# Folding the MLP gain of a streaming encoder into its up weights, and moving the row scaling to ScalarE

## The chip, the cores and the metric

The kernel runs on one core of one Trainium2 chip. It is one program in one launch. The metric is device time in microseconds (us): the median of the runs of a kernel, with the lowest and highest shown beside it. One execution of each kernel was also recorded by the hardware profiler; times "in the trace" are counted from the start of that execution's span.

## The reference

One inference step of an encoder with two layers (an "A" layer with sliding-window attention, a "B" layer that attends over a shared K/V), for 1024 prompt tokens and 8 x 16 sample tokens, with a model width D of 1024 and an MLP width FF of 4096. Everything is float32. What the change touches is the MLP that ends each layer:

```python
def rmsnorm(x, g):
    y = x * rsqrt(mean(x * x, axis=-1, keepdims=True) + EPS)
    return y * g

def mlp(x, g_norm, w_up, w_down):
    return square(relu(rmsnorm(x, g_norm) @ w_up)) @ w_down

for layer in range(2):
    ...                                   # attention; its output a_p, a_s
    hp = hp + a_p @ w_o[layer]            # prompt rows
    hs = hs + a_s @ w_o[layer]            # sample rows
    hp = hp + mlp(hp, g_mlp[layer], w_up[layer], w_down[layer])
    hs = hs + mlp(hs, g_mlp[layer], w_up[layer], w_down[layer])
```

`g_mlp` has one gain for each of the 1024 channels. It multiplies the normalized row along its channels; the channels are also the rows of `w_up`.

## The kernel before

Rows of tokens are held in nine tiles of 128 tokens: 0 to 7 for the prompt, 8 (`ST`) for the sample tokens. Float32 products are made from float32r matrix multiplies: each operand is split into a rounded part and a remainder (`split`: a cast, on ScalarE as a rule, L109, then a subtraction, on VectorE as a rule, L115), and three multiplies (`mm3`, L727 to L729) stand for one.

Each layer has four stages.

1. `attention(layer)`: projections, scores, probabilities, values, and part of the output projection. At its step 10 a load is issued on SP that broadcasts the layer's `g_mlp` to 128 partitions (L1685, tile `gb`, 128x1024). Tiles named in `kept` get their norm at the end of this stage (L1730).
2. `wo_phase(layer)`, the row phase: the rest of the output projection (`ps_wo`, L157 to L159), the residual added in VectorE (L665), and `norm`: ScalarE sums the squares (L617), VectorE makes mean and EPS of it (L619), GpSimd takes the power -0.5 (L621), and VectorE multiplies the row in place by that number and by `gb` (L622). Then the rows are transposed for the MLP. The MLP of the prompt is multiplied by a Strassen-like scheme of seven products over quarters, so for each pair of row tiles (t, t + 4) GpSimd makes four sums and differences of half rows (`S`, L681 to L684), and `T` makes seven groups of four 128x128 transposes on TensorE (`turn`, L674) into one bank `ps_n` each, which ScalarE casts and VectorE subtracts into the operands `sx`. The row phase has four PSUM banks for `ps_wo` and three for `ps_n`.
3. `mlp_up`: 16 blocks of 256 columns of `w_up`. Per block two raw weight tiles (`raw[0]`, `raw[1]`, 128x4x256, upper and lower half of the channels) are loaded by SP (L755, three buffers), split into `wq`, combined in place on VectorE (L787 to L790) and split again. Seven products follow (`ps_x`, `ps_y`, `ps_z`), with the sample tokens' product (`ps_s`) in between. ScalarE copies `ps_x` out three times per block (L846, L851, L855) before the next product adds into the same bank. Block 0 runs in two halves of 256 tokens.
4. `mlp_down`: the second half of the MLP, with the same scheme.

The order of the instructions on each engine is laid out when the kernel is built, by a planner that simulates the whole program (`schedule_with_timeline_sim=True`); at run time each engine works its queue in order. `behind` adds a few orders by hand, and `follow` keeps the products of the MLP in order on TensorE.

SBUF places follow from the order in which pools open. `raw`, `wa` and `keep` (with `gb` and the sums `s0` to `s3`) lie low and stay from the attention through the row phase; the pools of `mlp_up` open in their place. The first `hc` tiles of `mlp_up` begin where the sums `s2` and `s3` lay.

The gains of the attention norms are already folded into their weights: `prep_gains` turns all five gain vectors, the two of `g_mlp` among them, into columns of the tile `gcol` (one column for each 128 channels), which `split_g` uses as a scale for each partition.

Of the kernel before, what the change touches and what calls it, by code (L numbers as in the profile page):

```python
# [8 lines left out]
F32 = mybir.dt.float32  # L9
F32R = mybir.dt.float32r  # L10
AF = mybir.ActivationFunctionType
ALU = mybir.AluOpType
# [4 lines left out]
P = 128  # L17
D = 1024
KC = D // P
# [56 lines left out]
class Build:  # L76
# [537 lines left out]
    def norm(self, small, junk, x):  # L614
        nc = self.nc
        ssq = small.tile([P, 1], F32, tag="mssq", name="mssq")
        nc.scalar.activation(junk, x, AF.Square, accum_out=ssq)  # L617
        ms = small.tile([P, 1], F32, tag="mms", name="mms")
        nc.vector.tensor_scalar(ms, ssq, 1.0 / D, EPS, ALU.mult, ALU.add)  # L619
        rs = small.tile([P, 1], F32, tag="mrs", name="mrs")  # L620
        nc.gpsimd.tensor_tensor(rs, ms, self.mhalf[:, 0:1], ALU.pow)  # L621
        return nc.vector.scalar_tensor_tensor(x, x, rs, self.gb, ALU.mult, ALU.mult)  # L622

    def wo_phase(self, layer, sx, x8, wo):
        nc = self.nc
        with ExitStack() as st:
            self.psum_pools(st, f"wo{layer}", dict(m=(4, 1), g=(3, 1)), dict(m="m", n="g"))
            work = self.pool(st, f"wow{layer}")
            small = self.pool(st, f"wosm{layer}", 2)
            osp, xs = {}, {}  # L630
# [63 lines left out]
            z = 0  # L694
# [64 lines left out]
    def mlp_up(self, layer, sx, x8, rp, raw0):  # L759
        nc = self.nc  # L760
        tt = nc.vector.tensor_tensor
        with ExitStack() as st:
# [11 lines left out]
            def weights(b):  # L774
                raw = self.up_raw(layer, rp, b) if b else raw0
                quad = []
                for h in range(2):
                    q = [
                        take(f"q{b % 2}{v}") if h else rp[0].tile([P, 4, FB], F32R, tag=f"q{v}", name="wq")
                        for v in range(2)  # L780
                    ]
                    self.split(q[0], q[1], raw[h])
                    quad.append(q)
                b11, b12 = raw[0][:, :, 0:P], raw[0][:, :, P:FB]
                b21, b22 = raw[1][:, :, 0:P], raw[1][:, :, P:FB]
                t = b11, b22, b12, b21
                tt(t[0], b12, b11, ALU.subtract)  # L787
                tt(t[2], b22, b12, ALU.subtract)
                tt(t[1], b22, t[0], ALU.subtract)
                tt(t[3], b21, t[1], ALU.subtract)  # L790
                ts = [None] * 4
                for n in (1, 2, 0, 3):
                    w = take(f"t{b % 2}{n}")
                    self.split(w[:, 0], w[:, 1], t[n])
                    ts[n] = w[:, 0], w[:, 1]
                q = lambda h, n: [quad[h][v][:, :, n * P : n * P + P] for v in range(2)]
                return quad, [q(0, 0), q(1, 0), q(1, 1), ts[3], ts[0], ts[1], ts[2]]
# [77 lines left out]
            for b in range(NFB):  # L875
# [7 lines left out]
                s = [hp.tile([P, 512], F32, tag="h", name="hs", bufs=HB) for _ in range(3)]  # L883
# [284 lines left out]
    def run(self):  # L1168
        nc, tc = self.nc, self.tc
        I = self.ins  # L1170
# [7 lines left out]
        with ExitStack() as top:  # L1178
# [49 lines left out]
            for layer in range(2):  # L1228
                with ExitStack() as st:
                    low = st.enter_context(ExitStack())  # L1230
                    self.rawp = self.pool(low, f"raw{layer}", 2)
                    self.wa = [self.pool(low, f"wa{layer}")]
                    self.nw = 0
                    keep = self.pool(low, f"keep{layer}")
                    self.gb = keep.tile([P, D], F32, tag="gb", name="gb")
                    self.sums = lambda: [
                        keep.tile([P, 512], F32, tag=f"s{n}", name="s") for n in range(4)
                    ]
                    self.sums0 = self.sums()
                    self.kept = {}  # L1240
                    with ExitStack() as more:
                        self.wa.append(self.pool(more, f"wb{layer}"))
                        wo = self.attention(layer)
                    sx, x8, rp = self.up_pools(st, layer)
                    raw0 = self.up_raw(layer, rp, 0)
                    self.wo_phase(layer, sx, x8, wo)
                    low.close()
                    self.mlp_up(layer, sx, x8, rp, raw0)
                self.mlp_down(layer, y if layer else lambda t: self.xd[t])
# [24 lines left out]
    def attention(self, layer):  # L1274
        nc, I = self.nc, self.ins
# [17 lines left out]
        with ExitStack() as st:  # L1293
# [292 lines left out]
            def weave(*fs):  # L1586
                for z in zip(*fs):
                    run(z)
# [57 lines left out]
            wo = [None, None]  # L1646
# [34 lines left out]
            for s in range(2 * NT):  # L1681
                u = U(s)
                next(u)
                if s == 10:
                    nc.sync.dma_start(self.gb, I["g_mlp"][layer].partition_broadcast(P))  # L1685
                q, n = s + 2, s + 3
                f = work_of(2 * s)
                if s == 7:
                    f.insert(2, lambda: Q2(ST, 1))
                a, b, c, d = cfg["up"]  # L1690
# [17 lines left out]
                f = work_of(2 * s + 1)  # L1708
# [20 lines left out]
            for xt in self.kept.values():  # L1729
                n = self.norm(small, self.scratch([P, D], mybir.dt.bfloat16, "junk"), xt)  # L1730
# [76 lines left out]
```

## Time and profile before

| | |
|---|---|
| median of 3 runs | 2391.8 us |
| lowest and highest | 2388.46, 2393.51 us |
| the profiled execution, its own time | 2387.86 us |
| its span | 2386.1 us |
| granted TensorE clock over the span | 0.996 of full speed |
| TensorE (PE) busy | 2313.9 us, 97% |
| VectorE (DVE) busy | 1627.6 us, 68% |
| ScalarE (ACT) busy | 1216.5 us, 51% |
| GpSimd (POOL) busy | 540.8 us, 23% |

The span is what the profiler saw from the first to the last instruction; the execution's own time has 1.8 us around it. "Busy" counts the time in which at least one instruction ran on the engine; PEld is TensorE's loading of weights, which runs beside its multiplies. Windows are given as start:end in us of the trace. In a row of instructions, "x3" says that three were merged into one row.

### The profile page before, as it was taken

What the parts mean: (1) busy time and instruction counts of PE and PEld (TensorE: products, weight loads), DVE (VectorE), ACT (ScalarE), POOL (GpSimd) and SP (SyncE); (2) the same over time, 40 slices, a digit from 0 to 9 for tenths busy, and PEclk for the clock granted to TensorE, in tenths of its full rate; (3) what the DMA queues carried; (4) which work ended last, traced back from release to release, by engine and by line L of the source; (5) the groups of instructions that cost most, each with busy time, mean ns of one, the idle gap of its engine ahead of it and who ended that gap; (6) DMA issues with size and microseconds to landing.
All of it is one profiled execution on the core that took longest, in us unless ns stands there. A gap on an engine that the chain in (4) does not pass through costs nothing.

```text
span 2386.1 us, 33438 instructions
## 1 busy us (share of the span) xinstructions
PE 2313.9 (97%) x11621; PEld 1931.7 (81%) x11621; DVE 1627.6 (68%) x3002; ACT 1216.5 (51%) x2423; POOL 540.8 (23%) x828
## 2 busy tenths in 40 slices
PE   7998999899999999999999999998999999999999
PEld 6787877788888878888778788887888888888887
DVE  6788786655565776776577876877555565777674
ACT  3777674555555432332267666665555555323321
POOL 4334332311221100000333444444111211000000
PEclk9999999999999999999999999999999999999999
DMA  7335545343443964333653655554443445734332
GB/s 258 119 108 169 170 146 200 129 146 126 157 146 123 356 213 149 119 128 109 232 153 112 198 166 167 168 168 169 142 142 129 158 145 203 274 133 159 117 113 115
DMA packets 217529, 383.78 MB, mean 161 GB/s; under 512 B 50248, under 2 KB 124944, under 8 KB 210192
## 3 DMA queue, kind: packets, MB, share of 16 engines
q1 hardware_dynamic: 194288, 305.08, 38.9%
q0 software_dynamic: 21776, 71.84, 7.8%
q10 hardware_dynamic: 1296, 4.72, 0.5%
q8 instruction: 92, 1.51, 0.3%
q14 instruction: 77, 0.63, 0.1%
HBM read 245.42 MB, written 135.09 MB: 159 GB/s over the span
## 4 chain that ended last, share of the span: by engine, by line
PE 79%; DVE 7%; DMA 7%; ACT 3%; issue 2%; POOL 1%; SPq 1%; ACTq 0%; DVEq 0%; POOLq 0%
PE ps_x L727 9%; PE ps_x L729 9%; PE ps_x L728 9%; PE ps_y L729 7%; PE ps_y L728 7%; PE ps_y L727 7%; PE ps_mm L198 3%; PE ps_mm L200 3%; PE ps_mm L199 3%; PE ps_tr L305 2%; PE ps_mm L157 1%; PE ps_mm L158 1%; PE ps_mm L159 1%; PE ps_s L729 1%; PE ps_s L728 1%
## 5 line engine op out<-in xcount | busy, mean ns | idle before, releaser
L109 ACT CAST w<-r 128x2048 fp32r<-128x2048 f32 x56 | 107.1, 1913 | 325.2 <-PE ps_y L729 213.0
L727 PE MATMUL ps_x<-w,s 128*128 128x512 f32 x512 | 199.6, 390 | 4.2 <-DVE hc L866 2.1
L729 PE MATMUL ps_x<-w,s 128*128 128x512 f32 x512 | 199.4, 389 | 0.0
L728 PE MATMUL ps_x<-w,s 128*128 128x512 f32 x512 | 199.3, 389 | 0.0
L198 PE MATMUL ps_mm<-w,hh 128*128 128x512 f32 x432 | 172.5, 401 | 7.3 <-POOL w L166 3.2
L200 PE MATMUL ps_mm<-w,hl 128*128 128x512 f32 x432 | 172.1, 399 | 1.6 <-DVE hl L115 0.8
L199 PE MATMUL ps_mm<-w,hh 128*128 128x512 f32 x432 | 170.9, 397 | 1.3 <-DVE w L171 1.1
L109 ACT CAST s<-s 128x2048 fp32r<-128x2048 f32 x56 | 107.1, 1913 | 118.1 <-DMA s<-hd 109.3
L115 DVE TENSOR_TENSOR w<-r,w 128x2048 fp32r<-128x2048 f32 x56 | 128.2, 2290 | 51.0 <-ACT w L109 51.0
L727 PE MATMUL ps_x<-sx,w 128*128 128x512 f32 (+1 forms) x408 | 157.9, 387 | 3.9 <-ACT hc L846 3.0
L1033 DVE TENSOR_TENSOR x<-ps_y,x 128x512 f32<-128x512 f32 x136 | 92.4, 687 | 100.8 <-PE ps_y L729 100.8
L729 PE MATMUL ps_x<-sx,w 128*128 128x512 f32 (+1 forms) x408 | 154.2, 378 | 0.0
L728 PE MATMUL ps_x<-sx,w 128*128 128x512 f32 (+1 forms) x408 | 154.1, 378 | 0.0
L109 ACT CAST w<-ru 128x512 fp32r<-128x512 f32 (+1 forms) x160 | 110.0, 708 | 85.5 <-PE ps_y L728 32.0
L729 PE MATMUL ps_y<-w,s 128*128 128x512 f32 x384 | 149.5, 389 | 0.0
L727 PE MATMUL ps_y<-w,s 128*128 128x512 f32 x384 | 149.4, 389 | 0.0
L728 PE MATMUL ps_y<-w,s 128*128 128x512 f32 x384 | 149.4, 389 | 0.0
L115 DVE TENSOR_TENSOR s<-s 128x2048 fp32r<-128x2048 f32 x56 | 128.0, 2286 | 29.1 <-ACT s L109 28.9
L115 DVE TENSOR_TENSOR ptl<-ps_tr,pth 128x512 fp32r<-128x512 f32 x180 | 122.5, 685 | 24.1 <-ACT pth L109 17.8
L115 DVE TENSOR_TENSOR w<-ru,w 128x512 fp32r<-128x512 f32 (+1 forms) x160 | 126.5, 793 | 11.2 <-ACT w L109 11.1
L115 DVE TENSOR_TENSOR wq<-ru,wq 128x1024 fp32r<-128x1024 f32 x32 | 39.7, 1240 | 131.9 <-ACT wq L109 131.9
L109 ACT CAST pth<-ps_tr 128x512 fp32r<-128x512 f32 x180 | 104.9, 595 | 45.0 <-PE ps_tr L305 36.7
(280 smaller groups left out, 6579.7 us busy)
## 6 DMA issues: line engine op xcount, KB each, us to landing
s<-hd SPq DMA_DIRECT2D x56, 1024.0 KB, 4.7
ru<-in_w_up SPq DMA_DIRECT2D x64, 512.0 KB, 4.0
r<-in_w_down SPq DMA_DIRECT2D x32, 1024.0 KB, 5.8
hd<-hc POOLq DMA_DIRECT2D x128, 256.0 KB, 2.7
hd<-hs POOLq DMA_DIRECT2D x96, 256.0 KB, 2.5
x<-xd SPq DMA_DIRECT2D x41, 512.0 KB, 4.4
o<-oTd SPq DMA_DIRECT2D x52, 256.0 KB, 5.0
xd<-xo SPq DMA_DIRECT2D x18, 512.0 KB, 2.8
```

Of the source, the lines that this page charges most:

```text
L109: a = nc.scalar.copy(hi, src)
L115: return a, e.tensor_tensor(lo, src, hi.bitcast(F32), ALU.subtract)
L157: nc.tensor.matmul(ps, oh[:, k, :], w[:, 0, k, nn], start=(k == 0), stop=False)
L158: nc.tensor.matmul(ps, oh[:, k, :], w[:, 1, k, nn], start=False, stop=False)
L198: nc.tensor.matmul(ps, a, w[:, 0, k, :], start=(k == 0), stop=False)
L199: nc.tensor.matmul(ps, a, w[:, 1, k, :], start=False, stop=False)
L200: self.lp = nc.tensor.matmul(ps, b, w[:, 0, k, :], start=False, stop=(k == KC - 1))
L305: self.lp = nc.tensor.transpose(pt[:, i, :], get(i), self.ident)
L727: a = mm(ps, ah, bh, start=first, stop=False, skip_group_check=True)
L728: mm(ps, ah, bl, start=False, stop=False, skip_group_check=True)
L729: return a, mm(ps, al, bh, start=False, stop=last, skip_group_check=True)
L1033: tt(xs[t][:, N[n]], ps, xs[t][:, N[n]], ALU.add)
```

## The change

Four edits. The broadcast load of `g_mlp` and its tile `gb` go. `norm` no longer multiplies by the gain and by the row's factor on VectorE; ScalarE multiplies by the row's factor alone. The gain is multiplied into the raw up weights in place, in eight slices of 128x256 per block, before they are split: on GpSimd in block 0, on ScalarE in blocks 1 to 15. And `ps_n` in the row phase gets a fourth PSUM bank. Without `gb`, all that opens after `keep` lies 4 KB per partition lower.

```diff
@@ norm
-        return nc.vector.scalar_tensor_tensor(x, x, rs, self.gb, ALU.mult, ALU.mult)
+        return nc.scalar.activation(x, x, AF.Copy, scale=rs)
@@ wo_phase
-            self.psum_pools(st, f"wo{layer}", dict(m=(4, 1), g=(3, 1)), dict(m="m", n="g"))
+            self.psum_pools(st, f"wo{layer}", dict(m=(4, 1), g=(4, 1)), dict(m="m", n="g"))
@@ mlp_up, weights(b)
                 raw = self.up_raw(layer, rp, b) if b else raw0
                 quad = []
                 for h in range(2):
+                    for k in range(4):
+                        c = (2 + layer) * KC + h * 4 + k
+                        z, g = raw[h][:, k], self.gcol[:, c : c + 1]
+                        if b:
+                            nc.scalar.activation(z, z, AF.Copy, scale=g)
+                        else:
+                            nc.gpsimd.tensor_scalar(z, z, g, 1.0, ALU.mult, ALU.mult)
@@ run
-                    self.gb = keep.tile([P, D], F32, tag="gb", name="gb")
@@ attention
-                if s == 10:
-                    nc.sync.dma_start(self.gb, I["g_mlp"][layer].partition_broadcast(P))
```

## Rows read from the trace of the kernel before

**Rows 1.** The page: busy time of each engine, share of the span, instructions.
```profile
PE 2313.9 (97%) x11621; PEld 1931.7 (81%) x11621; DVE 1627.6 (68%) x3002; ACT 1216.5 (51%) x2423; POOL 540.8 (23%) x828
```

**Rows 2.** Windows by stage: busy us of each engine, clock, DMA share, GB/s.
```profile
core 0: us, PE busy (x) PEld busy (x) DVE busy (x) ACT busy (x) POOL busy (x), PEclk, DMA share, GB/s
...
490.00:803.00 313.00, 311.94 (x1545) 263.93 (x1544) 176.52 (x249) 174.61 (x280) 61.97 (x115) 1.00 0.45 160
...
50.00:330.00 280.00, 267.84 (x1477) 222.67 (x1475) 223.52 (x728) 202.60 (x590) 106.61 (x192) 0.99 0.47 146
...
1200.00:1560.00 360.00, 348.52 (x1915) 288.21 (x1914) 274.89 (x784) 244.64 (x682) 147.43 (x207) 1.00 0.53 162
...
425.00:450.00 25.00, 18.27 (x127) 15.01 (x125) 22.03 (x34) 16.41 (x31) 10.65 (x9) 1.00 0.34 120
...
1650.00:1680.00 30.00, 21.61 (x133) 17.82 (x132) 27.43 (x42) 19.05 (x36) 12.53 (x11) 0.89 0.30 106
...
0.00:50.00 50.00, 39.48 (x170) 32.29 (x171) 30.62 (x62) 14.13 (x29) 23.66 (x33) 1.00 0.71 255
```

**Rows 3.** TensorE's waits, 425 to 450 and then 1650 to 1680: total, times, longest.
```profile
PE ps_n L674 <- DVE sx L115: 3.4, 4, 1.9
PE ps_x L727 <- ACT hc L846: 1.4, 1, 1.4
...
PE ps_n L674 <- DVE sx L115: 6.1, 6, 2.4
```

**Rows 4.** VectorE's timeline in both tails: its row multiplications.
```profile
429.26 1.28 DVE L622 SCALAR_TENSOR_TENSOR x<-x,mrs,gb 128x1024 f32<-128x1024 f32 x1 [0.97 <-POOL mrs L621]
...
436.25 1.72 DVE L622 SCALAR_TENSOR_TENSOR x<-x,mrs,gb 128x1024 f32<-128x1024 f32 x1
...
1653.32 1.28 DVE L622 SCALAR_TENSOR_TENSOR x<-x,mrs,gb 128x1024 f32<-128x1024 f32 x1 [0.73 <-POOL mrs L621]
...
1655.33 2.28 DVE L622 SCALAR_TENSOR_TENSOR x<-x,mrs,gb 128x1024 f32<-128x1024 f32 x1
...
1663.10 1.29 DVE L622 SCALAR_TENSOR_TENSOR x<-x,mrs,gb 128x1024 f32<-128x1024 f32 x1 [0.94 <-DMA xd<-x]
```

**Rows 5.** GpSimd's timeline in the second tail: two sums of one pair.
```profile
1655.26 1.27 POOL L681 TENSOR_TENSOR s<-x 128x512 f32<-128x512 f32 x1
1656.61 2.14 POOL L682 TENSOR_TENSOR s<-s,x 128x512 f32<-128x512 f32 x1
```

**Rows 6.** Groups by form, whole span: busy us, mean ns of one, idle before.
```profile
L622 DVE SCALAR_TENSOR_TENSOR x<-x,mrs,gb 128x1024 f32<-128x1024 f32 x14 | 21.9, 1567 | 2.8 <-POOL mrs L621 1.7 <-DMA xd<-x 0.9
...
L109 ACT CAST wq<-ru 128x1024 fp32r<-128x1024 f32 x32 | 33.5, 1047 | 26.0 <-PE ps_s L729 25.9
...
L109 ACT CAST w<-ru 128x512 fp32r<-128x512 f32 x128 | 76.4, 621 | 48.6 <-DVE ru L790 23.6 <-DVE ru L787 22.1 <-DVE ru L789 2.8
...
L168 ACT ACTIVATE w<-raw,gcol 128x512 fp32r<-128x512 f32 x8 | 5.3, 720 | 0.0
...
L582 ACT ACTIVATE sp<-sp,li 128x256 f32<-128x256 f32 x16 | 8.2, 512 | 4.9 <-DVE li L397 4.8
...
L384 POOL TENSOR_SCALAR p<-p,li 128x256 f32<-128x256 f32 x112 | 53.7, 500 | 65.1 <-DVE li L397 52.3 <-ACT p L376 5.7 <-DVE nm L371 4.7
```

**Rows 7.** Timelines of ScalarE and TensorE in one up block: two copies, the products behind.
```profile
581.73 0.59 ACT L846 COPY hc<-ps_x 128x512 f32<-128x512 f32 x1 [0.19 <-DMA hd<-hs]
...
592.79 0.59 ACT L855 COPY hc<-ps_x 128x512 f32<-128x512 f32 x1 [0.50 <-PE ps_x L729]
...
584.25 0.39 PE L727 MATMUL ps_x<-sx,w 128*128 128x512 f32 x1
...
595.45 0.48 PE L727 MATMUL ps_x<-sx,w 128*128 128x512 f32 x1
```

**Rows 8.** The instructions that write or read `gb`: the load's issue on SP.
```profile
L1685 SPq DMA_DIRECT2D gb<-in_g_mlp x2: 332/336/340, 28.0 to 1166.3; - x2
```

## The prediction

> **What bounds the kernel now.** I read the page's engine shares first. TensorE is busy 2313.9 of 2386.1 us, ScalarE about half [rows 1]. So there are 72.2 us in which TensorE does not work, and a change that leaves its matrix multiplies alone can win only out of these, or add to them. The second view is the windows by stage. In the steady part of the first MLP's up projection TensorE lacks 1.1 us in 313; in the two attention stretches 12.2 us in 280 and 11.5 us in 360; but in the 25 us at the end of the first row phase it lacks 6.7 us, and in the 30 us at the end of the second 8.4 us [rows 2]. I call these two stretches the tails: the output projection runs out, and the transposes of the rows and their sums (L674) feed the first block of the MLP. In the tails VectorE is the full engine: 22.0 of 25 us, and 27.4 of 30, where ScalarE has 16.4 and 19.1 [rows 2]. The third view, TensorE's waits in the tails, names the same engine: the transposes wait for a bank of `ps_n` that VectorE's subtraction (L115) has still to read, 3.4 us and 6.1 us; the longest wait on another engine is one for ScalarE's first copy of `ps_x`, 1.4 us in each (its row reads the same in both tails) [rows 3]. In the second tail TensorE's granted clock is 0.89 of full speed, a mean of its two levels of 2.4 and 1.2 GHz; in the first it is 1.00 [rows 2]. The fourth view is VectorE's own order there: between the evictions stand the row multiplications of L622, two in the first tail (1.28 and 1.72 us), three in the second (1.28, 2.28 and 1.29 us) [rows 4]. Those are what the change takes away.
>
> **The change part by part.**
>
> *The row multiplication goes from VectorE to ScalarE.* There are 18 in all; 14 of them average 1567 ns [rows 6]. Most run while TensorE is fed by the projection, and give back nothing. The five in the tails stand in a queue that has almost no gaps: 1.28 + 1.72 = 3.0 us in the first, 1.28 + 2.28 + 1.29 = 4.85 us in the second. I count 7.85 us. No row shows the new form, 128x1024 with a scale per partition. It lies between a ScalarE cast of the same shape without one, 1047 ns, and twice the scaled 128x512, 2 x 720 ns; I take 1047 plus the 99 ns by which the scaled 128x512 exceeds the plain cast (720 - 621), 1.14 us [rows 6]. Then ScalarE would have 16.4 + 2 x 1.14 = 18.7 us in a tail of 25 - 3.0 = 22.0 us, and 19.1 + 3 x 1.14 = 22.5 us in one of 30 - 4.85 = 25.2 us. It fits, with the second tail at nine tenths. The bounds: nothing, if ScalarE sets the pace there; and all of TensorE's idle time in both tails, 15.1 us, if VectorE was the whole cause. What a clock that no longer falls would give back in the second tail stays inside this bound.
>
> The long ones among these multiplications show a collision. The 2.28 us one starts at 1655.33, beside a GpSimd sum that runs from 1655.26 for 1.27 us, and GpSimd's next sum takes 2.14 us in place of 1.27 [rows 4, 5]. Each seems to have waited about 1 us for the other. The Trainium skill (GPSIMD Engine Reference, section 8, Key points) has it that GpSimd shares its SBUF interfaces with VectorE and contends with VectorE instructions that have two SBUF inputs, as L622 has (`x` and `gb`); by that rule the sums behind it, from which four of every seven transposes are made, should also come about 1 us earlier in the second tail, and the sum would be 8.8 us instead of 7.85. I leave this 1 us out of the value, since the sums still meet other two-input work of VectorE, and keep it inside the 15.1 us.
>
> *The gain moves into the up weights.* In blocks 1 to 15 of each layer ScalarE multiplies eight slices of 128x256 in place: 240 instructions. The same form is measured at 512 ns [rows 6], so 4.1 us per block of some 22 us and 123 us in all. In the steady stretch ScalarE has 174.6 of 313 us [rows 2]; some 14 blocks bring it to 232 us, 74%. I cost this at nothing on TensorE. The cover is ScalarE's idle 138 us there; and as TensorE lacks 1.1 us in the stretch, nothing that the split weights feed is late now. If the cover is gone, what is late next is the copy of `ps_x` (L846, L851, L855), since the next product writes the same bank. L846 ends at 582.32 (581.73 + 0.59) and its product starts at 584.25, 1.93 us later; L855 ends at 593.38 and its product starts at 595.45, 2.07 us later [rows 7]. One scaling ahead of a copy is 0.5 us and disappears in this; the rival below counts from when it doesn't.
>
> In block 0 GpSimd does the same work: 8 slices per layer at 500 ns [rows 6], 4.0 us. GpSimd is busy 10.7 of 25 us and 12.5 of 30 us in the tails [rows 2], so it has the room. I take nothing; if all eight stood ahead of a tail's sums it would cost 4.0 us in that layer. Queued behind them would be the next row's power (L621) and the sums.
>
> *The fourth bank.* The transposes wait 3.4 and 6.1 us for one of three banks [rows 3]. A fourth lets TensorE run one transpose group further ahead, but each bank still needs the same VectorE subtraction, about 0.6 us apart, and VectorE has hardly a gap. Alone I take it at nothing. Its bounds are 0 and the 9.5 us of these waits; they overlap with the 15.1 us and aren't added to it.
>
> *The broadcast load of the gain.* One issue on SP and 512 KB per layer go; the issue takes 336 ns [rows 8]. Nobody waits for `gb`. At the 255 GB/s of the first 50 us [rows 2] the transfer is worth 2.1 us of the queues, in stretches where the weight loads decide; I take 0, with a gain of 4.1 us over both layers as the far end.
>
> *Places in SBUF.* Without `gb` what opens after `keep` moves 4 KB down. The first `hc` tile of the MLP then lies no longer on the sums of the row phase but on a row tile, which is done earlier; this may take the 1.4 us wait for L846 [rows 3] away, in each layer. I take 0; 2.8 us is inside the 15.1.
>
> The sum: 0 (weights) + 0 (block 0) + 0 (bank) + 0 (load) - 7.85 = -7.85 us. The profiled execution took 2387.86 us, 1.8 us more than its span of 2386.1, so 2380.0 for an execution like it. It lies 3.9 us below the median of the runs, 2391.8; taken from the median, **2384 us** (-0.33%). What this measurement can tell from no change is about 0.2%, 4.8 us.
>
> **The rivals.**
>
> *ScalarE takes VectorE's place in the tails: no gain.* It carries the cast of every transpose group already and would have 22.5 of 25.2 us, in program order, with a row's scaling queued behind casts and casts behind the scaling. For it: after the subtraction, ScalarE is the next releaser in TensorE's waits [rows 3]. Against it: a scaled row costs ScalarE 1.14 us and cost VectorE 1.28 to 2.28 us. The tails keep their length or give back up to 3 us: 2389 to 2392. The Trainium skill (ScalarE: Activation LUTs, Rules for kernel authors) speaks for this side: plain multiplies belong on VectorE and not on ScalarE. By that rule the move would cost time; here the rows say otherwise of this one form, 1047 ns for a ScalarE pass over 128x1024 against 1.28 us or more for the two-tensor one on VectorE [rows 4, 6].
>
> *ScalarE's queue in the up projection: slower.* If ScalarE runs the eight scalings as one run ahead of a copy of `ps_x`, or stands before one whose raw weights have not landed, TensorE waits. Eight are 4.1 us, less the slack of 1.93 us: 2.2 us per block, over 30 blocks 65 us, so some 2450. Four in a run, one half of a block's weights, are 2.05 us and cost 0.1 us per block, 3.6 us in all. To end above 2396.6 the up projection must lose 7.85 + 4.8 = 12.7 us, 0.42 us per block: a copy that is late by 1.93 + 0.42 = 2.35 us, so five scalings in a run. Against it: they are separate short instructions with nothing that ties them together, and ScalarE's gaps are spread over the block.
>
> *The planner lays everything out anew.* The order on each engine is planned over the whole program, and a load less and shifted buffers can change it in the attention as well, where TensorE lacks 12.2 and 11.5 us [rows 2]. Half as much again would be +12 us, so 2396 with the gain; the other way is as possible.
>
> **How the numbers follow.** The tails shrink by over 4.8 us: 0.60. ScalarE takes over: 0.24, of which 0.04 still faster and 0.20 within the bound. The queue in the up projection: 0.10, slower. The planner's disturbance as the larger part: 0.06, half within the bound, half slower. Faster 0.64, same 0.23, slower 0.13. The low end is 2391.8 - 15.1 = 2376.7, a little lower for the loads, 2376; at the top the range holds the whole case of no gain (2391.8) and 1 us of block 0's or the planner's cost, 2393. The likeliest case alone spans 2377 to 2387.
>
> **What would show it.** Right: no VectorE instruction of 128x1024 in the tails, a ScalarE one of about 1.14 us; TensorE's idle time in the two tails down from 15.1 to some 7 us, its waits on L115 shorter; GpSimd's sums at 1.3 us and none above 2; TensorE lacking about 1 us in a stretch of 313 us of the up projection as now, with ScalarE at some 74%. Wrong: the transposes waiting on ScalarE's cast instead; waits of TensorE on L846, L851 or L855 in every block; or a gain in the tails beside new idle time in the attention.

## The result, and the profile after

The change made the kernel slower: 2397.15 us, the median of 10 runs (2392.42 to 2401.16), against 2388.58 us for 10 runs of the kernel before. The ratio is 1.0036, with a 95% interval of 1.0027 to 1.0044. The forecast was 2384.0 us and faster.

The profiled execution of after took 2392.42 us, with a span of 2390.6; that is the lowest of its ten times, so the profile shows only about half of the loss. Profiles of the kernels below lie up to 6 us from their medians too, and what is read from them by stage has to be held against the medians.

In after, lines behind L777 stand 7 lower: the copies L846, L851 and L855 are L853, L858 and L862, and L789 is L796. The busy line of after's page, which answers to [rows 1]:

```profile
PE 2314.3 (97%) x11621; PEld 1931.5 (81%) x11621; DVE 1603.9 (67%) x2984; ACT 1318.6 (55%) x2681; POOL 543.6 (23%) x844
```

ScalarE has 258 instructions and 102 us more, VectorE 24 us less, TensorE the same work. The groups by form (busy us, mean ns of one, idle time before):

```profile
L782 ACT ACTIVATE ru<-ru,gcol 128x256 f32<-128x256 f32 x240 | 102.6, 498 | 40.4 <-DMA ru<-in_w_up 39.2 <-DVE hc L873 1.3
...
L622 ACT ACTIVATE x<-x,mrs 128x1024 f32<-128x1024 f32 x14 | 15.9, 1161 | 6.4 <-POOL mrs L621 4.0 <-DMA xd<-x 2.5
...
L784 POOL TENSOR_SCALAR ru<-ru,gcol 128x256 f32<-128x256 f32 x16 | 7.8, 503 | 6.0 <-DMA ru<-in_w_up 6.0
```

The three new forms cost what [rows 6] led to expect: 498 ns for 512, 1161 for 1140, 503 for 500. But before the scalings ScalarE sat idle for 40.4 us in all, 39.2 of it until the load of the weights it was to scale. The windows of [rows 2] again, in after:

```profile
490.00:803.00 313.00, 311.94 (x1543) 263.27 (x1541) 176.02 (x250) 208.72 (x377) 61.57 (x115) 1.00 0.45 159
425.00:450.00 25.00, 19.89 (x131) 16.95 (x130) 18.74 (x31) 21.44 (x41) 10.98 (x10) 0.93 0.36 127
1650.00:1680.00 30.00, 23.20 (x142) 20.04 (x141) 19.28 (x33) 20.93 (x36) 11.73 (x11) 0.92 0.18 66
1600.00:1650.00 50.00, 42.30 (x226) 34.38 (x226) 31.35 (x64) 35.66 (x80) 25.59 (x32) 0.97 0.59 195
```

In the steady up projection TensorE has the same 311.94 us as before. In the tails VectorE is relieved (22.0 to 18.7 us, 27.4 to 19.3) and TensorE lacks 5.1 and 6.8 us where it lacked 6.7 and 8.4, but ScalarE is now fuller there than VectorE (21.4 and 20.9 us). The first tail has lost its full clock: 0.93, where it was 1.00. And the 50 us ahead of the second tail lack 7.7 us, where the kernel before lacks 2.9 (and nofold, a kernel below without the scaling of weights, 6.2). TensorE's waits from 1600 to 1710 us:

```profile
PE ps_n L674 <- DVE sx L115: 5.4, 2, 4.4
PE ps_n L674 <- ACT x L622: 4.4, 1, 4.4
PE ps_x L727 <- ACT hc L858: 1.1, 1, 1.1
```

Two single waits of 4.4 us have come, where [rows 3] had many of at most 2.4. The first lies near 1640 us, in the middle of the row phase; the second is for the last row's scaling on ScalarE.

To place the loss I cut each profile at three marks per layer: the first product of the row phase's output projection, the first sample product of block 0 (`ps_s`), and the first product of `mlp_down` into `ps_y` from a sum (`ps_y<-w,s`), which comes some 16.5 us behind that stage's first product in each kernel. For the second row phase of after, and then of the same kernel without any scaling of weights (the run nofold below), the marks are these rows of TensorE's timeline:

```profile
1632.21 0.50 PE L157 MATMUL ps_wo<-w,oh 128*128 128x512 f32 x1
...
1693.54 0.28 PE L727 MATMUL ps_s<-wq,sx 128*128 128x256 f32 x1
```

```profile
1629.85 0.50 PE L157 MATMUL ps_wo<-w,oh 128*128 128x512 f32 x1
...
1682.96 0.28 PE L727 MATMUL ps_s<-wq,sx 128*128 128x256 f32 x1
```

That is 61.3 us in after and 53.1 without the scaling. All kernels of the study (times are medians; "row" from the first mark to the second, "up" from the second to the third, us, by layer, one profile each):

| kernel | time | ratio to before, 95% | row 0 | up 0 | row 1 | up 1 |
|---|---|---|---|---|---|---|
| before | 2388.6 to 2390.1 | | 71.9 | 360.3 | 57.4 | 359.8 |
| after | 2397.2 | 1.0036 [1.0027, 1.0044] | 72.2 | 361.2 | 61.3 | 360.6 |
| bank4 | 2387.3 | 0.9997 [0.9985, 1.0009] | 73.3 | 360.0 | 56.1 | 360.9 |
| nofold | 2383.3 | 0.9970 [0.9957, 0.9982] | 69.0 | 359.9 | 53.1 | 360.8 |
| rows_dve | 2398.2 | 1.0038 [1.0024, 1.0053] | 76.9 | 361.9 | 59.9 | 362.1 |
| pad4k | 2394.0 | 1.0024 [1.0012, 1.0035] | 71.7 | 361.6 | 59.0 | 362.6 |
| fold0 | 2392.6 | 1.0019 [1.0008, 1.0030] | 69.1 | 359.8 | 62.7 | 359.8 |
| fold1 | 2387.8 | 0.9995 [0.9985, 1.0006] | 72.1 | 359.9 | 58.6 | 359.8 |
| fold2 | 2388.0 | 0.9994 [0.9983, 1.0005] | 70.5 | 362.2 | 54.2 | 363.3 |
| fold_pool | 2396.7 | 1.0032 [1.0022, 1.0041] | 72.7 | 360.4 | 64.7 | 359.8 |
| late1 | 2394.5 | 1.0019 [1.0009, 1.0029] | 70.6 | 362.0 | 61.3 | 362.2 |
| late0 | 2399.0 | 1.0038 [1.0025, 1.0051] | 71.5 | 361.7 | 64.6 | 362.7 |
| oback_late0 | 2401.8 | 1.0051 [1.0036, 1.0065] | 71.7 | 361.8 | 62.2 | 362.7 |
| all3 | 2397.9 | 1.0036 [1.0022, 1.0049] | 70.4 | 360.8 | 62.9 | 363.3 |
| plate | 2396.0 | 1.0029 [1.0018, 1.0040] | 71.6 | 361.1 | 61.1 | 362.7 |
| act0 | 2397.0 | 1.0038 [1.0024, 1.0051] | 75.0 | 360.8 | 58.9 | 361.8 |
| dve0 | 2394.7 | 1.0027 [1.0016, 1.0037] | 73.8 | 362.2 | 58.7 | 362.7 |
| dve0_late1 | 2389.4 | 0.9999 [0.9989, 1.0009] | 70.6 | 362.3 | 56.3 | 363.3 |
| best | 2386.3 | 0.9983 [0.9974, 0.9992] | 70.5 | 360.1 | 56.1 | 360.0 |
| bestv | 2385.4 | 0.9988 [0.9979, 0.9997] | 71.0 | 360.6 | 55.7 | 359.9 |

What lies between a layer's up projection and the next row phase (the first `mlp_down` and the second attention) took from 809 to 818 us in these profiles, though none of the edits is there: the planner's order differs, and I found no single cause. A difference of a few us between two medians can come from there.

### The profile page after: what moved, and what is told of

It reads as the page before. It is cut to its first block, busy times and chain, and to the rows that moved or that the text cites. A ratio compares the mean times of both kernels' runs of the same rounds, so it can differ in the third digit from the quotient of the medians.

```text
span 2390.6 us, 33675 instructions
## 1 busy us (share of the span) xinstructions
PE 2314.3 (97%) x11621; PEld 1931.5 (81%) x11621; DVE 1603.9 (67%) x2984; ACT 1318.6 (55%) x2681; POOL 543.6 (23%) x844
## 5 line engine op out<-in xcount | busy, mean ns | idle before, releaser
L782 ACT ACTIVATE ru<-ru,gcol 128x256 f32<-128x256 f32 x240 | 102.6, 498 | 40.4 <-DMA ru<-in_w_up 39.2
```

Source lines behind the costliest of these rows:

```text
L782: nc.scalar.activation(z, z, AF.Copy, scale=g)
```

## The experiments

### Which part of the change costs

Edits: bank4 is the kernel before with `g=(4, 1)`; nofold is after without the loop over `k`; rows_dve and pad4k are after with

```diff
@@ norm (rows_dve)
-        return nc.scalar.activation(x, x, AF.Copy, scale=rs)
+        return nc.vector.tensor_scalar(x, x, rs, None, ALU.mult)
@@ run (pad4k)
                     keep = self.pool(low, f"keep{layer}")
+                    keep.tile([P, D], F32, tag="gb", name="gb")
```

bank4: 

> The kernel before with the fourth bank for the transposes alone; gain, rows and places as before. Theory P (places: without the 4 KB of gb the up weights load earlier on SP, ahead of the row phase's own loads, and the second row phase loses): nothing of P is here, so 2388.6 within 3 us. Theory S (ScalarE's queue: the scalings of raw weights, which wait for their load, and the row scaling stand ahead of what TensorE waits for): nothing of S either, the same number. If the bank itself orders transposes ahead of the projection and so makes the loss, 2393 or more, with TensorE's gap of over 4 us in the second row phase.

nofold: 

> The changed kernel without the scaling of the up weights: the gain of the MLP's norm is left out altogether, so 240 ScalarE and 16 GpSimd instructions are gone; row scaling on ScalarE, fourth bank and places as changed. Theory S: the loss goes with them, 2386 to 2390, and in the first MLP block no wait of TensorE on the second copy of ps_x. Theory P: the gap in the second row phase stays, 2393 to 2397.

rows_dve: 

> The changed kernel, but the row is multiplied by its factor on VectorE (one tensor, no gain); fold, bank and places as changed. If ScalarE's chain of three rows at the end of the second row phase makes a large part of the loss: the 4.4 us wait of TensorE on the row scaling goes, 2391 to 2393. Theory P: the first gap (VectorE held by a late load) stays, some 4 us of the loss. If the weights' scaling alone is the cause: 2396 to 2398.

pad4k: 

> The changed kernel with an unused 4 KB tile in gb's place, so that every other tile lies where it lay before; no load into it. Theory P: the up weights load after the row phase's own loads again, the gap of 4.4 us behind VectorE in the second row phase goes, 2390 to 2393. Theory S: 2396 to 2398, as the changed kernel.

The bank alone is worth nothing that can be measured. Everything but the fold gains 5.9 us (2389.2 to 2383.3), and the fold takes 13.9 us (2383.3 to 2397.2): the loss is the fold's, with the order that the planner makes of it. In nofold the tails are as forecast (busy us in the columns of [rows 2]):

```profile
425.00:450.00 25.00, 20.71 (x153) 18.41 (x152) 18.30 (x30) 18.87 (x37) 8.47 (x8) 1.00 0.36 125
1650.00:1680.00 30.00, 26.16 (x191) 23.27 (x190) 20.73 (x35) 23.56 (x44) 9.21 (x9) 1.00 0.29 105
```

TensorE lacks 4.3 and 3.8 us there, 8.1 in place of 15.1, at the full clock. The row phases are 2.9 and 4.3 us shorter than before; by after they are 0.3 and 3.9 us longer. With the fold in place it makes no difference to the time whether ScalarE or VectorE multiplies the row factor (rows_dve; in its one profile the first row phase is 4.7 us longer than in after and the second 1.4 us shorter), and the place of the tiles makes at most some 3 us (pad4k), which the intervals don't separate.

### Which block's scaling costs

fold0, fold1 and fold2 put a condition on the loop: `for k in range(4) if b == 0 else ():`, and `b == 1`, `b >= 2`. fold_pool replaces `if b:` by `if b < 0:`.

fold0: 

> The gain is multiplied into the weights of block 0 alone (eight slices per layer, on GpSimd) and left out of blocks 1 to 15. Without any scaling the changed kernel took 2383.3 us, with all of it 2397.2 us. Theory G (the loss is made by block 0: GpSimd's eight slices, 8 x 0.48 us, stand between the load of block 0's weights and its casts and sums, which then fall later into the crowded row phase): 2392 to 2397. Theory Q (the loss is made by block 1: its slices stand in ScalarE's queue in the row phase, waiting for their load, ahead of the casts, row scalings and copies that TensorE waits for): 2382 to 2386. Theory U (the steady part of the up projection pays for ScalarE's 4 us per block): 2382 to 2386.

fold1: 

> The gain is multiplied into the weights of block 1 alone (eight slices per layer, on ScalarE) and left out of the other fifteen blocks. Theory Q (block 1's slices in ScalarE's queue in the row phase): 2391 to 2397, and the copies L853 or L858 late by 1 to 2 us in the first block. Theory G (block 0): 2382 to 2386. Theory U (the steady part): 2382 to 2386.

fold2: 

> The gain is multiplied into the weights of blocks 2 to 15 alone (224 instructions of ScalarE, none of them in the row phase) and left out of blocks 0 and 1. Theories G and Q (the loss is made in the row phase, by block 0 or by block 1): 2382 to 2386, as without any scaling. Theory U (the steady part pays): 2391 to 2397, with TensorE lacking some 5 us more in each layer's up projection.

fold_pool: 

> All 256 slices are scaled by GpSimd, none by ScalarE. Theory Q (ScalarE's queue): 2383 to 2389, since ScalarE's queue is then as without scaling. Theory G (block 0's chain through GpSimd): 2392 to 2397, and more, if block 1's chain through GpSimd is late in the same way. Theory U (ScalarE in the steady part): 2383 to 2389.

No single theory holds. Against nofold, block 0 costs 9.3 us, block 1 4.5, the fourteen others 4.7; together they cost 13.9, less than the sum of 18.5. (These are medians of different rounds. By the ratios to before, each uncertain by some 4 us, it is 11.7, 6.0, 5.7 and 15.8 us.) The table says where; its profiles of fold1 and fold2 lie 3.8 and 2.3 us above their medians. Block 0's price lies wholly in the second row phase (62.7 against 53.1; the first is 69.1 against 69.0). Block 1's lies in both (72.1 and 58.6). That of the others lies in the up projections (2.3 and 2.5 us more) and 1.5 and 1.1 us of the row phases. Moving all to GpSimd frees the up projections (360.4 and 359.8) and makes the second row phase worse.

For block 1, ScalarE's timeline of after at the start of the first up projection, and then nofold's:

```profile
443.05 0.38 ACT L853 COPY hc<-ps_x 128x256 f32<-128x256 f32 x1
444.05 1.71 ACT L782 ACTIVATE ru<-ru,gcol 128x256 f32<-128x256 f32 x4 [0.61 <-DMA ru<-in_w_up]
445.79 1.04 ACT L109 CAST w<-ru 128x1024 fp32r<-128x1024 f32 x1
...
447.06 0.35 ACT L858 COPY hc<-ps_x 128x256 f32<-128x256 f32 x1
...
449.00 1.71 ACT L782 ACTIVATE ru<-ru,gcol 128x256 f32<-128x256 f32 x4 [1.28 <-DMA ru<-in_w_up]
450.62 0.34 ACT L862 COPY hc<-ps_x 128x256 f32<-128x256 f32 x1
```

```profile
441.26 0.39 ACT L846 COPY hc<-ps_x 128x256 f32<-128x256 f32 x1
442.16 1.06 ACT L109 CAST w<-ru 128x1024 fp32r<-128x1024 f32 x1 [0.52 <-DMA ru<-in_w_up]
...
444.45 0.35 ACT L851 COPY hc<-ps_x 128x256 f32<-128x256 f32 x1
...
446.59 0.37 ACT L855 COPY hc<-ps_x 128x256 f32<-128x256 f32 x1 [1.46 <-PE ps_x L729]
```

In block 0's first half the copies come 2 to 3 us apart in nofold, and TensorE needs each before its next product. In after four scalings of block 1, 1.71 us, stand ahead of the second copy (its other four ran at 407.95 us), and four of block 2 ahead of the third; fold1 has none at that place. Each group first waits for its load. The three copies come 1.8, 2.6 and 4.0 us later than in nofold, but the first 1.8 us are there before any of the scalings shown. And TensorE did not wait longer for the copies. Its waits from 425 to 460 us, in nofold and then in after:

```profile
PE ps_x L727 <- ACT hc L846: 1.4, 1, 1.4
PE ps_x L727 <- ACT hc L851: 1.4, 1, 1.4
```

```profile
PE ps_x L727 <- ACT hc L853: 1.4, 1, 1.4
PE ps_x L727 <- ACT hc L858: 1.0, 1, 1.0
```

With 0.4 us for the third copy in after, that is 2.8 us in both. What differs is the products behind the first wait: most start 0.21 us apart in after and 0.12 us in nofold, so TensorE reached the second copy later too. In the first layer, then, the copies are late, but no longer wait is seen. In the second layer it waits 1.0 and 1.1 us for the first two copies in after and 1.4 and 1.9 in fold1, against 1.4 and 0.5 in nofold. There the same place ends the chain of work (after, start and us):

```profile
1675.46 0.61 DVE ru L796
1676.13 3.68 DMA ru<-in_w_up
1679.89 1.71 ACT ru L782 x4
...
1682.01 1.04 ACT w L109
1683.05 0.28 ACT hc L858
1683.37 0.39 PE ps_x L727
```

Read upwards: the product waits for a copy, the copy stands behind a cast and four scalings, these wait for a load, and the load waits until L796 has used up one of the three raw buffers.

Waits are only a part of these prices. The same profiles, read from the first mark to the second, split each row phase into TensorE's idle time, its busy time and its granted clock (us; one profile each):

| kernel | row 0: idle | busy | clock | row 1: idle | busy | clock |
|---|---|---|---|---|---|---|
| before | 6.7 | 65.2 | 1.00 | 8.5 | 48.9 | 0.94 |
| after | 5.5 | 66.7 | 0.98 | 12.4 | 48.9 | 0.92 |
| nofold | 4.3 | 64.7 | 1.00 | 6.7 | 46.4 | 0.97 |
| fold0 | 4.3 | 64.8 | 1.00 | 12.3 | 50.4 | 0.86 |
| fold1 | 4.6 | 67.5 | 0.95 | 9.5 | 49.2 | 0.91 |
| late0 | 4.9 | 66.6 | 0.98 | 12.6 | 52.0 | 0.84 |
| plate | 5.1 | 66.5 | 0.98 | 10.2 | 50.9 | 0.89 |
| act0 | 7.2 | 67.8 | 0.98 | 10.3 | 48.6 | 0.91 |
| dve0 | 5.0 | 68.8 | 0.93 | 10.5 | 48.2 | 0.91 |
| best | 5.4 | 65.1 | 1.00 | 8.6 | 47.5 | 0.94 |

The second row phase of nofold, after and fold0, in the columns of [rows 2]:

```profile
1629.90:1683.00 53.10, 46.40 (x298) 40.44 (x298) 36.25 (x59) 37.73 (x70) 21.56 (x19) 0.97 0.47 156
1632.20:1693.50 61.30, 48.93 (x297) 43.15 (x297) 37.61 (x59) 42.79 (x82) 26.04 (x27) 0.92 0.40 136
1630.30:1693.00 62.70, 50.37 (x298) 45.08 (x298) 38.03 (x59) 38.44 (x70) 26.01 (x27) 0.86 0.39 132
```

TensorE has the same work in each (297 or 298 records, 303 in before), so more busy time is work that ran slower. Of fold0's 9.6 us over nofold in the second row phase 5.6 are idle time and 4.0 are slower work; of after's 8.2 us, 5.7 and 2.5. Of fold1's 3.1 us in the first row phase only 0.3 are idle time, and 2.8 are slower work. It is not these profiles alone: the granted clock over a whole execution averages 0.993 in after's ten runs, 0.996 in nofold's six, and 0.995 in the kernel before.

### VectorE's queue in the second row phase: a theory that fell

At 1640.96 us in after, VectorE waits 2.08 us for a load of the attention's output (L322); a sum of block 0's weights (L794, 1.75 us) comes next, and behind both the evictions that TensorE waits 4.4 us for. I took this queue for the cause of block 0's price, and put the evictions ahead by hand.

```diff
@@ late1: block 1's scalings behind block 0's third copy
-                            nc.scalar.activation(z, z, AF.Copy, scale=g)
+                            y = nc.scalar.activation(z, z, AF.Copy, scale=g)
+                            if b == 1:
+                                self.behind(self.cp, y)
...
                 a = nc.scalar.copy(v[3], X)
+                if not with_sample:
+                    self.cp = a
@@ late0: L794 behind a residual addition (self.adds holds those of L665)
-                tt(t[0], b12, b11, ALU.subtract)
+                d = tt(t[0], b12, b11, ALU.subtract)
+                if layer and not b:
+                    self.behind(self.adds[-4], d)
@@ oback_late0: late0, and L322 behind an eviction (self.ev holds T's; load_halves returns its sum)
+                d = self.load_halves(layer, 1, t, o, second, nc.vector)
+                if layer and t == 7:
+                    self.behind(self.ev[0][5], d)
```

late1: 

> The changed kernel, with block 1's eight scalings on ScalarE put behind the third copy of block 0's first half (L862 in the rows of after), so that no copy stands behind a scaling that waits for its load. Theory Q (block 1's scalings in ScalarE's queue take back some 3 us of the first row phase and 1 us of the second, by the runs with block 1 alone): the wait of TensorE for L858 down from 1.0 and 1.1 us to under 0.5, first row phase (first output product to first sample product) 69 to 70 us in place of 72.2, time 2391 to 2394. Rival (any new order costs this much, whatever it is): stage times as in the changed kernel, 2395 to 2399.

late0: 

> The changed kernel, with block 0's first VectorE sum (L794) in the second layer put behind the third last but one residual addition of the row phase, so that it no longer stands ahead of two evictions that TensorE waits for. Theory G (GpSimd's scalings of block 0 make this sum later than the load of the attention's last output half, so it falls behind the combination that waits for that load, and the evictions behind both): the 4.4 us wait of TensorE for ps_n near 1640 us falls by the sum's 1.75 us to some 2.7, time 2393 to 2396. Rival (the sum is no part of it): wait 4.4 us, 2395 to 2399.

oback_late0: 

> As the run before, and the combination that waits for the load (L322, tile 7 of the second layer) put behind the two evictions as well. Theory G: the wait near 1640 us falls from 4.4 to under 1 us, the second row phase (first output product to first sample product) from 61.3 to 54 to 57 us, time 2390 to 2393. Rival (the transposes wait for something else, the head of VectorE's queue only looks like it): second row phase 59 us or more, 2395 to 2399.

all3 (all of these): 

> The changed kernel with all three orders of this call. If the fold's cost lies in these two places of the queues alone, row phases of 69 to 70 and 54 to 57 us, and 2385 to 2389, so that it is at least as fast as the kernel before (2389) and near the one without any scaling (2383). If the 4 us of ScalarE per block cost something everywhere, or the planner's new order as such does, 2391 or more.

The theory fell. The queue was changed as meant, and in late0 the wait near 1640 us did fall to 2.8 us, as expected and as in nofold (2.7). But the second row phase got no shorter in any of the three (64.6, 62.2, 62.9): in late0 TensorE's idle time there is 12.6 us, as in after (12.4), and its work ran slower, at a clock of 0.84 against 0.92. In oback_late0 a wait of 4.6 us has come under another name (lines there stand 4 lower):

```profile
PE ps_n L678 <- DVE mms L619: 4.6, 1, 4.6
```

late1 shortened the first row phase by 1.6 us, less than the 2 to 3 us expected: TensorE's wait for the second copy stayed at 1.4 us, where under 0.5 was expected, and four scalings of block 2 still stand ahead of the third copy, for which it waits 1.1 us. Its time, 1.0019, is lower than after's 1.0036, with intervals that meet.

### GpSimd's queue in the second row phase

The transposes that start behind that wait in oback_late0 are those of GpSimd's sums (`s`); in after, those behind the 4.4 us are of the rows themselves. GpSimd's timeline in after, and then in nofold:

```profile
1634.05 1.84 POOL L784 TENSOR_SCALAR ru<-ru,gcol 128x256 f32<-128x256 f32 x4 [0.80 <-DMA ru<-in_w_up]
1635.86 1.29 POOL L684 TENSOR_TENSOR s<-xo,s 128x512 f32<-128x512 f32 x1
1637.12 2.30 POOL L681 TENSOR_TENSOR s<-x 128x512 f32<-128x512 f32 x1
1639.40 1.84 POOL L784 TENSOR_SCALAR ru<-ru,gcol 128x256 f32<-128x256 f32 x4
1641.20 1.70 POOL L682 TENSOR_TENSOR s<-s,x 128x512 f32<-128x512 f32 x1
1642.86 1.73 POOL L683 TENSOR_TENSOR s<-x 128x512 f32<-128x512 f32 x1
1644.55 1.27 POOL L684 TENSOR_TENSOR s<-x,s 128x512 f32<-128x512 f32 x1
```

```profile
1630.97 1.30 POOL L684 TENSOR_TENSOR s<-xo,s 128x512 f32<-128x512 f32 x1
1632.22 1.30 POOL L681 TENSOR_TENSOR s<-x 128x512 f32<-128x512 f32 x1
1636.18 1.37 POOL L682 TENSOR_TENSOR s<-s,x 128x512 f32<-128x512 f32 x1 [2.65 <-PE ps_n L674]
1637.51 1.71 POOL L683 TENSOR_TENSOR s<-x 128x512 f32<-128x512 f32 x1
1639.18 1.73 POOL L684 TENSOR_TENSOR s<-x,s 128x512 f32<-128x512 f32 x1
```

The eight scalings stand between the sums of the first two pairs. The second pair's last sum ends 13.6 us after the row phase's mark in after (1645.82 - 1632.21), 11.1 in nofold (1640.91 - 1629.85). In the first row phase the scalings ran before any sum, and cost nothing.

```diff
@@ plate: block 0's scalings behind the second pair's last sum (self.sm holds these)
-                            nc.gpsimd.tensor_scalar(z, z, g, 1.0, ALU.mult, ALU.mult)
+                            y = nc.gpsimd.tensor_scalar(z, z, g, 1.0, ALU.mult, ALU.mult)
+                            if layer:
+                                self.behind(self.sm[1], y)
@@ act0: all on ScalarE
-                        if b:
+                        if b >= 0:
@@ dve0: block 0 on VectorE
-                            nc.gpsimd.tensor_scalar(z, z, g, 1.0, ALU.mult, ALU.mult)
+                            nc.vector.tensor_scalar(z, z, g, 1.0, ALU.mult, ALU.mult)
```

plate: 

> The changed kernel, with block 0's eight scalings on GpSimd in the second layer put behind the last sum (L684) of the second pair of row tiles; nothing else is moved by hand. Theory GP (GpSimd's in-order queue holds the sums, and so the transposes, behind the scalings): second row phase 53 to 57 us in place of 61.3, the 4.4 us wait of TensorE near 1640 us gone or under 2 us, time 2388 to 2392. Theory W (the weights of block 0 come too late through the longer chain, wherever it runs): second row phase 61 us or more, since they now come later still, 2397 or more.

act0: 

> The changed kernel with block 0's scalings on ScalarE like all others, so that GpSimd has only its sums and powers. Theory GP: second row phase 54 to 58 us, GpSimd's sums of the second pair ended some 11 us after the phase begins, time 2388 to 2393 (ScalarE has 4 us more in each row phase, of which the first may lose 1 us). Theory W: 60 us or more, 2395 or more.

dve0: 

> The changed kernel with block 0's scalings on VectorE. Theory GP: second row phase 54 to 58 us, time 2388 to 2393. Theory W: 60 us or more, 2395 or more. If VectorE is already full there (it has eight more instructions of 128x256), the evictions wait and it lies between.

dve0_late1 (dve0 and late1): 

> As the run before, and block 1's scalings on ScalarE behind the third copy of block 0's first half. Theory GP with ScalarE's queue as the rest of the cost: first row phase 69.5 to 71 us, second 53 to 57, time 2385 to 2390. If the later place of block 1's weights costs as much in the up projection as it gives back (the run late1 had 0.8 to 1.6 us more there), 2388 to 2393 as the run before.

GpSimd's queue is a part, not the whole. Off GpSimd, the second row phase falls from 61.3 to 58.9 and 58.7 us, which is what block 1 alone has (58.6 in fold1), and the 4.4 us wait for a row's scaling is gone. It is gone in plate too, but plate, where the sums are early again, stays at 61.1 (its GpSimd; L785 is L784):

```profile
1639.92 1.26 POOL L685 TENSOR_TENSOR s<-x,s 128x512 f32<-128x512 f32 x1
1641.16 4.97 POOL L785 TENSOR_SCALAR ru<-ru,gcol 128x256 f32<-128x256 f32 x8
1646.10 0.56 POOL L621 TENSOR_TENSOR mrs<-mms,mhalf 128x1 f32<-128x1 f32 x1
```

The eight now stand ahead of the rows' powers, and the weights come later still. TensorE's idle time is 2.1 us less than in after; what took the gain back is its clock, 0.89 against 0.92, with 1.9 us more of busy time. Whether the powers or the later weights brought that about, I can't say. In the first row phase the other engines are worse places for block 0 than GpSimd (75.0 and 73.8 against 72.2). With block 1 later as well, dve0_late1 reaches 70.6 and 56.3 and the time of the kernel before; what it loses is now in the up projections, 2.0 and 3.5 us above before, in a profile that is the slowest of its 12 runs, 4.9 us above their median. TensorE's waits there, 470 to 790 us and then 1700 to 2022 (L855 is L853):

```profile
PE ps_x L727 <- ACT hc L855: 1.6, 2, 1.1
...
PE ps_x L727 <- ACT hc L855: 2.4, 2, 2.0
```

Two late copies in each, of some 48; the kernel before has one such wait, of 0.3 us. Ahead of the latest, at 1798.25 us, ScalarE waits 2.95 us for a load and then runs four scalings.

### A version that beats both

best scales blocks 1 to 15 on GpSimd, idle in the up projection, with block 1 behind the same copy, and block 0 where it was cheapest in each layer. bestv has block 0 on VectorE in both.

```diff
@@ best, with late1's self.cp
-                        if b:
-                            nc.scalar.activation(z, z, AF.Copy, scale=g)
-                        else:
-                            nc.gpsimd.tensor_scalar(z, z, g, 1.0, ALU.mult, ALU.mult)
+                        e = (nc.vector if layer else nc.gpsimd) if b == 0 else nc.gpsimd
+                        y = e.tensor_scalar(z, z, g, 1.0, ALU.mult, ALU.mult)
+                        if b == 1:
+                            self.behind(self.cp, y)
```

best: 

> The whole change, with other engines for the scalings: block 0 on GpSimd in the first layer (where the slices run before the sums) and on VectorE in the second, blocks 1 to 15 on GpSimd, block 1 behind the third copy of block 0's first half. Theory S (ScalarE's in-order queue is the rest of the fold's cost): first row phase 69 to 71 us, second 55 to 58, up projections 360 to 361 each, time 2384 to 2388, faster than both kernels. Rival (the rest lies in the planner's new order of the attention and the row phases): 2388 to 2393.

bestv: 

> As the run before, but block 0 of the first layer on VectorE too. Theory S: up projections 360 to 361 us, row phases as in the run with block 0 on VectorE and block 1 later (70.6 and 56.3), time 2385 to 2389. Rival: 2388 to 2393.

best takes 2386.3 us, ratio 0.9983 [0.9974, 0.9992]: faster than before by 0.17%, at the edge of what can be told, and than after by some 0.5% (0.9983 against 1.0036). The up projections are back at 360.1 and 360.0 us, as theory S had it. Its steady stretch:

```profile
490.00:803.00 313.00, 311.94 (x1543) 263.59 (x1542) 185.14 (x248) 172.96 (x280) 127.25 (x212) 1.00 0.46 160
```

The same 311.94 us of TensorE, with the work in GpSimd's idle time. Its row phases, 70.5 and 56.1, keep 1.4 and 1.3 us of nofold's 2.9 and 4.3. bestv's median is lower by 1.0 us; the ratios don't separate the two. Nor do they separate best from bank4 (0.9997 [0.9985, 1.0009]), whose second row phase is 56.1 us as well; that best beats the fourth bank alone is not shown.

## Why the prediction was wrong

The tails were read rightly. "I count 7.85 us", 3.0 and 4.85; without the fold the row phases gave back 2.9 and 4.3. The row on ScalarE takes 1161 ns where 1.14 us was taken. TensorE's idle time in the tails fell to 8.1 us, "some 7" by the prediction. The fourth bank is worth nothing, as costed. But that the gain came out so near the sum is in part luck: of the 7.2 us that nofold's row phases gave back, 4.2 are idle time and 3.0 are work that ran faster, mostly in the second one at a clock of 0.97 in place of 0.94, which the sum had left out.

What I hadn't seen is why the row became cheap. Without the gain as a second tensor, the row costs 1127 ns on VectorE too (rows_dve, same form and count, against 1567 in [rows 6]). How much of nofold's gain is the change of engine was not tried.

The step that failed is the next one: "I cost this at nothing on TensorE. The cover is ScalarE's idle 138 us there". The cover is real for blocks 2 to 15 in the steady stretch, and the stretch did keep its 311.94 us. But blocks 0 and 1 are prepared in the row phases and at the very start of the up projection, so their 32 slices in both layers lie outside the stretch whose idle time was to cover them. There it counts what stands behind a slice in its engine's queue, not a share of busy time, and the sum had no term for it: of the 11.4 us that after's row phases have more than nofold's (3.2 and 8.2), block 1 alone has 3.1 and 5.5 and block 0 alone 0.1 and 9.6 (they don't add). And not all of it is waiting: 6.9 us of the 11.4 are idle time, 4.5 are work at a lower clock.

For block 0 the prediction named the mechanism and its price: "if all eight stood ahead of a tail's sums it would cost 4.0 us in that layer", with the power and the sums behind them, and took nothing. They stood among the sums, in one layer, at 1634 to 1641 us, ahead of the windows that I had called the tails; and alone they cost 9.6 us there, not 4.0: 5.6 us of idle time and 4.0 us of slower work. A wait of 3.2 to 4.5 us for a row's scaling goes with them: in the second row phase each kernel has it that scales block 0 on GpSimd among the sums and the rows on ScalarE, and no other has one above 0.6 us. How the scalings make the rows late, no run shows by itself.

The rival "ScalarE's queue in the up projection" had the mechanism for block 1 word for word (a scaling that "stands before one whose raw weights have not landed"), with a chance of 0.10. Its price was sought in every block, as a copy late by 2.35 us; in after the copies were late in one block per layer, by 1.8 to 4.0 us in the first. As a wait it is seen only in the second layer, where TensorE waits 0.6 us longer for the second copy, but 0.4 us less for the first (in fold1 1.4 us longer for the second); in the first layer the price is slower work. The slack of [rows 7], 1.93 us, is that of a full block, and block 0 runs in halves, with copies 2 to 3 us apart. In the later blocks too TensorE waited for such copies, 1.6 and 2.4 us per layer in dve0_late1, but 0.5 and 0.2 us in after.

The other rival, that ScalarE takes VectorE's place in the tails, is half true: VectorE's waits went, and a wait of 4.4 us for the row on ScalarE came, but only with block 0's scaling among GpSimd's sums; nofold has no wait for a row above 0.6 us. The third, that the planner's new order costs time in the attention, is not what happened: what lies between the first up projection and the second row phase took 813.9 us in before and 812.7 in after, and the first row phase starts at 386.4 and 386.1 us.

Four things stay open: what lowered TensorE's clock in the row phases; why block 0 and block 1 together cost less than the sum of the two alone; what of block 0's price is the sums, the powers or the later weights; and what moves the first `mlp_down` and the second attention by several us from one order to another.

## What to carry to other kernels

Work put on an idle engine is free only where its first and last pieces also fall into the idle time: price the pieces at the edges of a loop by the stretch in which they run, and name what stands behind each in that engine's queue. An operation that waits for a load should not stand ahead of work that the bound engine needs; give it an explicit place behind that work, or an engine that nobody waits for in that stretch. When a change has several parts, run it once without each: here the gain was real, and another part paid it away. And before a longer stretch is put down to waits, split it into idle and busy time: here 4.5 of 11.4 us were the same work at a lower clock.

## What the runs showed of the hardware

- In after's first tail the granted clock is 0.93, a mean of TensorE's levels of 2.4 and 1.2 GHz, where before and nofold have 1.00: behind the 1.4 us wait for L853 products of 128x256 start 0.21 us apart, and behind the same wait in nofold 0.12 us. So a wait of that length does not lower the clock by itself; what did, no run shows. The work of the second row phase took 46.4 us at a clock of 0.97 (nofold) and 52.0 us at 0.84 (late0).
- GpSimd's scaling of 128x256 takes 503 ns in block 0 (16 of them) and a mean of 651 ns in best, where 248 run, most of them beside VectorE's work in the up projection; VectorE is busy 185.1 us there, 9.1 us more than in after. Yet TensorE is as busy there as before, 311.94 us.
- Beside VectorE's work one of GpSimd's sums takes 2.30 us (L681 in after), where others take 1.27 [rows 5]. The Trainium skill (GPSIMD Engine Reference, section 8, Key points) has GpSimd contend with VectorE's two-input instructions; the rows agree, and in nofold, where L681 took 1.30, it was VectorE's split of the weights beside it that took 2.02 us in place of 1.22.
